# New duration estimates in the clock that writes a trunk kernel's program order

## The chip, the cores and the metric

The kernel runs on one core of a Trainium2 chip. The core's engines run side by side, each through its own instructions in the order in which the program holds them: TensorE (PE) multiplies matrices and writes to PSUM, VectorE (DVE), ScalarE (ACT) and GpSimd (POOL) work on elements, and SyncE (SP) issues DMA transfers. They wait for each other with semaphores. The metric is the device time of one execution in microseconds (us), as the median of several runs. A profiled execution stands beside them: its span runs from the first to the last instruction, and its own time is a little longer than the span.

## The reference

Two layers of an encoder trunk on 512 tokens of 1024 channels, in float32. Each layer is, in short:

```
h = rms_norm(x); proj = h @ w_in          # split into latents, GQA q/k/v, pool channels, 3 gates
o_mla  = latent attention (8 heads, 96-wide q and k, RMS norm per head, rotary part)
o_gqa  = grouped-query attention (8 heads, 2 kv heads, 64 wide, RMS norm per head, rotary)
o_pool = (centred means over 2/4/8/16 tokens - token) @ w_pool * pool_scale
merged = sum over branches of sigmoid(gate_b) * (o_b @ w_branch_b)
x = x + merged @ w_out
u = depthwise_conv3(rms_norm(x) @ w_up) + bias     # 2 * 2816 channels
x = x + (silu(u_gate) * u_val) @ w_down
```

## The kernel before, in words

**Number format.** Every large product is made of three matmuls. Each operand is split into a rounded high part and a low part (ACT makes hi, then DVE or POOL makes lo = x - hi), and high x high, high x low and low x high are added in PSUM. So each weight piece of 128 x 512 costs one DMA share, one ACT copy (wh) and one subtraction (wl). `w_split` (line 302) writes these two, and `wnext` (line 333) keeps them LA = 2 pieces ahead of the matmuls.

**Stages of a layer.** The input projection runs as latents, pool channels, GQA queries, then GQA keys and values. Then comes the GQA attention, with the pool branch's gates and branch products mixed in, as well as the MLA queries and keys; then the MLA attention, mixed with the GQA branch's gates and products and the MLA values; then the MLA branch's gates and products, the output projection, the up-projection with the convolution (`up_evac`, line 1300), and the down-projection.

**The planner's clock.** The program order is not fixed by the loops alone. While the Python code writes the program, `Clock` (line 118) simulates it. Each matmul moves the clock's `now` on by its length. Work behind a matmul is given as a `chain` (line 168): a list of steps, each written into the program when the simulated clock reaches the end of the step before. `took` (line 133) books a cost on an engine: it starts at the later of now (plus a semaphore's delay) and the time at which that engine is free. `Engine` (line 189) wraps the calls to DVE, ACT and POOL and gives each a cost of a fixed part plus so much for each element of a row: `_two` (line 211) is the cost of instructions with two inputs and of reductions, and `tensor_scalar`, `tensor_copy` and `reciprocal` (lines 226 to 234) have their own. `done` and `need` mark results and move the clock to them. None of these costs is an instruction; they only decide what is written when, and so in what order each engine finds its instructions.

Three decisions hang on the clock:

- `pick` (line 317) gives the subtraction of a weight piece (bias W_BIAS = 2.54) or of a probability block (P_BIAS = 1.16) to DVE if DVE is free early enough, otherwise to POOL. `copy` (line 455) chooses between ACT and DVE.
- In `attention` (line 1021) a plan holds, for each head, the positions of its steps: transposes of the query (`t_q`, `t_pair`) and key (`t_k`), the four row-maximum products (`s_max`, line 1098, matmul ps_S, then DVE's reduction nm), the row of maxima (`m_row`), the probabilities (`probs`: matmul ps_ST, exponential pe, its high part ph and low part pl) and the products with the values (`av_hi`, `av_lo`, PSUM bank AV). The position of step p says how many units of filler (gates and branch products, three to six matmuls each) go ahead of it: `fill.upto(target)`.
- Beyond that target, `waiting` (line 1243) asks the clock whether the step's inputs and PSUM bank are ready. As long as they aren't, further units of filler are written first, up to SLACK = 35 units over the target:

```
fill.upto(target)
while fill.done < target + SLACK and waiting(fn, *args) and fill.step():
    pass
fn(*args)
```

PSUM has eight banks: two each for `acc` (projections and filler), `ST` and `AV`, one each for `S` and `mi`.

**Inverse square roots.** `rsqrt_steps` (line 406) makes 1/sqrt on DVE for the norms: one bit operation and three Newton steps of three instructions, ten instructions on rows of 8 or 32 elements, written as one block (`go`). Seven such blocks stand in a layer (two for the token norms, one each for the latents, the GQA queries and keys, the MLA queries and the MLA keys).

## Time and profile before

| | |
|---|---|
| median of 3 runs | 1695.26 us (1694.22 to 1695.61) |
| profiled execution | 1693.48 us, span 1691.7 us |
| mean granted TensorE clock | 0.995 |
| busy: PE, DVE, ACT, POOL | 1649.7, 946.2, 775.4, 962.6 us |
| PE busy, GQA attention of layer 1 (100 to 220 us) | 109.27 of 120.00 us |
| PE busy, MLA attention of layer 1 (242 to 370 us) | 127.88 of 128.00 us |
| PE busy, up-projection of layer 1 (442 to 729 us) | 287.00 of 287.00 us |

A row of the timeline gives start, length, engine, line, operation, tiles (out<-in) and, in brackets, the idle time before it and who ended it. A row of waits gives the total, the number and the longest. A row of stages gives the stretch, its length, then the busy time and the number of instructions of PE, PEld (weight loads), DVE, ACT and POOL, the granted clock as a share of full speed, the DMA share and GB/s. A row of groups gives busy us and the mean ns of one instruction. Most instructions bear the line of the helper that records them: L341 is a matmul, L216 and L220 are two-input instructions, L224 a reduction, L209 an ACT instruction.

### The profile page before, as it was taken

Reading aid. Unit: us, or ns where it says so; the run is one execution under the profiler, and the core shown is the slowest. Engines: PE = TensorE matmul, PEld = TensorE weight load, DVE = VectorE, ACT = ScalarE, POOL = GpSimd, SP = SyncE. Lnnn points to the kernel's source line nnn. Section 1 sums busy time; section 2 is a strip of 40 time slices with the busy share of each in tenths; the row PEclk is TensorE's granted clock in tenths of the full one; section 3 lists DMA queues with packets and bytes.
Section 4 is the critical chain, followed back from the end, with each engine's and each line's share of the span. In section 5 each row is a group of like instructions: output and inputs, shape, how many; then the busy total and the mean of one; then the engine's idle time right before and its main releaser. Section 6 shows DMA issues by size and latency. Waiting matters only on the chain.

```text
span 1691.7 us, 20364 instructions
## 1 busy us (share of the span) xinstructions
PE 1649.7 (98%) x7360; PEld 1336.5 (79%) x7360; DVE 946.2 (56%) x1520; ACT 775.4 (46%) x1361; POOL 962.6 (57%) x759
## 2 busy tenths in 40 slices
PE   8989989999999999999999998999999999999999
PEld 7777667778888888888887786777888888888887
DVE  7776966643357666630157769666433666667100
ACT  5357645653344444432334575456434444444221
POOL 4435645764566656655544466556645665666543
PEclk9999999999999999999999999999999999999999
DMA  4221111113323232333332211111233222222331
GB/s 172 91 72 57 56 48 50 38 63 112 125 88 96 92 100 90 98 109 116 100 106 79 81 44 57 62 38 38 81 115 116 88 100 99 88 97 90 112 119 56
DMA packets 44596, 145.40 MB, mean 86 GB/s; under 512 B 5072, under 2 KB 6352, under 8 KB 44496
## 3 DMA queue, kind: packets, MB, share of 16 engines
q1 hardware_dynamic: 44352, 144.10, 25.7%
q8 instruction: 58, 0.95, 0.2%
q14 instruction: 42, 0.34, 0.1%
q10 hardware_dynamic: 144, 0.01, 0.0%
HBM read 139.90 MB, written 4.19 MB: 85 GB/s over the span
## 4 chain that ended last, share of the span: by engine, by line
PE 89%; DVE 6%; issue 2%; ACT 1%; POOL 1%; DMA 1%; SPq 0%; POOLq 0%; ACTq 0%; DVEq 0%
PE ps_acc L341 40%; PE ps_ST L341 23%; PE ps_AV L341 22%; PE ps_S L341 2%; PE ps_mi L345 1%; PE ps_mi L341 1%; DVE MQ L216 1%; POOL wl L216 1%; DVE yt L220 1%; DVE rp L216 1%; DVE nm L224 1%; DVE osum L236 0%; DVE ssm L224 0%; DVE tabg L216 0%; DMA raw<-w 0%
## 5 line engine op out<-in xcount | busy, mean ns | idle before, releaser
L216 POOL TENSOR_TENSOR wl<-raw,wh 128x512 fp32r<-128x512 f32 (+1 forms) x514 | 680.4, 1333 | 493.5 <-ACT wh L209 437.1
L209 ACT ACTIVATE wh<-raw 128x512 fp32r<-128x512 f32 (+3 forms) x522 | 313.7, 607 | 189.7 <-PE ps_ST L341 87.8
L220 DVE SCALAR_TENSOR_TENSOR a<-u,prm,a 128x512 f32<-128x512 f32 x176 | 242.3, 1377 | 79.8 <-ACT a L209 74.2
L341 PE MATMUL ps_acc<-HH,wh 128*128 128x512 f32 x592 | 236.2, 399 | 5.0 <-DVE XM L220 4.4
L341 PE MATMUL ps_acc<-HH,wl 128*128 128x512 f32 x592 | 234.9, 397 | 0.0
L341 PE MATMUL ps_acc<-HL,wh 128*128 128x512 f32 x592 | 234.9, 397 | 0.0
L216 POOL TENSOR_TENSOR pl<-pe,ph 128x512 fp32r<-128x512 f32 x109 | 143.1, 1313 | 114.2 <-ACT ph L209 77.9
L341 PEld LDWEIGHTS ps_acc<-HH,wh 128*128 128x128 f32 x592 | 112.5, 190 | 33.2 <-ACT wh L209 4.9
L341 PEld LDWEIGHTS ps_acc<-HH,wl 128*128 128x128 f32 x592 | 112.3, 190 | 26.3
L341 PEld LDWEIGHTS ps_acc<-HL,wh 128*128 128x128 f32 x592 | 112.5, 190 | 25.4
L209 ACT ACTIVATE pe<-ps_ST 128x512 f32<-128x512 f32 x128 | 76.1, 594 | 115.9 <-PE ps_ST L341 114.4
L224 DVE TENSOR_REDUCE nm<-ps_S 128x1 fp32r<-128x512 f32 x128 | 87.8, 686 | 55.5 <-PE ps_S L341 55.2
L341 PE MATMUL ps_AV<-HH,wh 128*128 128x512 f32 x288 | 113.8, 395 | 0.0
L341 PE MATMUL ps_AV<-HH,wl 128*128 128x512 f32 x288 | 113.7, 395 | 0.0
L341 PE MATMUL ps_AV<-HL,wh 128*128 128x512 f32 x288 | 113.7, 395 | 0.0
L216 POOL TENSOR_TENSOR al<-a,ah 128x512 fp32r<-128x512 f32 x44 | 58.1, 1321 | 84.8 <-ACT ah L209 58.5
L341 PE MATMUL ps_ST<-HH,wh 128*128 128x512 f32 x240 | 94.9, 395 | 0.0
L341 PE MATMUL ps_ST<-HH,wl 128*128 128x512 f32 x240 | 94.8, 395 | 0.0
L341 PE MATMUL ps_ST<-HL,wh 128*128 128x512 f32 x240 | 94.7, 395 | 0.0
L209 ACT ACTIVATE a<-u,prm 128x512 f32<-128x512 f32 x88 | 71.7, 815 | 27.6 <-DVE u L216 27.3
L209 ACT ACTIVATE ah<-a 128x512 fp32r<-128x512 f32 x44 | 27.8, 631 | 117.5 <-DVE u L240 112.0
L209 ACT ACTIVATE a<-a 128x512 f32<-128x512 f32 x44 | 27.8, 632 | 115.4 <-DVE u L240 115.4
(339 smaller groups left out, 3551.2 us busy)
## 6 DMA issues: line engine op xcount, KB each, us to landing
raw<-w SPq DMA_DIRECT2D x228, 512.0 KB, 3.4
raw<-w SPq DMA_DIRECT2D x13, 384.0 KB, 2.9
XM<-x SPq DMA_DIRECT2D x16, 256.0 KB, 3.8
raw<-w SPq DMA_DIRECT2D x6, 448.0 KB, 3.3
xsp<-XM SPq DMA_DIRECT2D x8, 256.0 KB, 2.0
XM<-xsp SPq DMA_DIRECT2D x8, 256.0 KB, 3.1
out<-XM SPq DMA_DIRECT2D x8, 256.0 KB, 2.4
raw<-w SPq DMA_DIRECT2D x4, 432.0 KB, 3.0
```

The lines of the kernel that those rows point to most:

```text
L209: return self.eng.activation(out, in_, func, **k)
L216: return self.eng.tensor_tensor(out, *a)
L220: return self.eng.scalar_tensor_tensor(out, *a)
L224: return self.eng.tensor_reduce(out, in_, *a, **k)
L341: PE.matmul(o, lhsT=lhsT, rhs=rhs, start=start, stop=stop)
L345: PE.transpose(o, src, ident)
```

## The change

All edits are to the planner's estimates. DVE instructions whose data inputs all lie in SBUF are booked with a wait for POOL: if POOL is booked beyond DVE's start, DVE starts up to 0.62 us later, and POOL's booking moves back by DVE's cost. POOL's two-input instruction gets 0.033 us more, POOL's `tensor_scalar` a cost of its own, the reciprocal less for each element, and each inverse square root 1.2 us more. The constants W_BIAS, P_BIAS, SLACK and the plan's positions stay as they are.

```
-    def took(self, engine, cost):
+    def took(self, engine, cost, port=False):
         start = self.now + (0.0 if self.source is None else 0.13 if self.source == engine else self.SEM)
-        self.free[engine] = max(start, self.free.get(engine, 0.0)) + cost
+        start = max(start, self.free.get(engine, 0.0))
+        if port:
+
+            pool = self.free.get("Pool", 0.0)
+            if pool > start:
+                start += min(0.62, pool - start)
+                self.free["Pool"] = max(pool, start) + cost
+        self.free[engine] = start + cost
...
-    def _count(self, ap, per, fixed):
+    def _count(self, ap, per, fixed, *ins):
...
-        self.ck.took(self.kind, fixed + per * n)
+        port = self.kind == "DVE" and len(ins) > 0 and all(x.space == bass.MemoryType.SB for x in ins)
+        self.ck.took(self.kind, fixed + per * n, port)
...
-    def _two(self, out):
-        self._count(out, *((0.002145, 0.127) if self.kind == "Pool" else (0.00105, 0.07)))
...
+    def _two(self, out, *ins):
+        self._count(out, *((0.002145, 0.16) if self.kind == "Pool" else (0.00105, 0.07)), *ins)
...
-    def tensor_scalar(self, out, *a):
-        self._count(out, 0.00055, 0.07)
...
+    def tensor_scalar(self, out, x, *a):
+        self._count(out, *((0.0043, 0.2) if self.kind == "Pool" else (0.00055, 0.07)), x)
...
     def tensor_copy(self, out, in_, psum=False):
-        self._count(out, 0.00105 if psum else 0.00053, 0.07)
+        self._count(out, 0.00105 if psum else 0.00053, 0.07, in_)
...
     def reciprocal(self, out, in_):
-        self._count(out, 0.0084, 0.07)
+        self._count(out, 0.0066, 0.07)
...
             for to in (y, y, a):
                 newton(to)
+            ck.free["DVE"] += 1.2
+            ck.fin = ck.free["DVE"]
```

`tensor_tensor` and `scalar_tensor_tensor` pass their two data inputs on to `_two`; `tensor_reduce` passes none, so that it never waits for POOL in the clock.

More of the change, by code (lines that the diff above doesn't have):

```diff
@@ L209, in activation, with tensor_tensor, scalar_tensor_tensor @@
         return self.eng.activation(out, in_, func, **k)
-    def _two(self, out):
-        self._count(out, *((0.002145, 0.127) if self.kind == "Pool" else (0.00105, 0.07)))
-    def tensor_tensor(self, out, *a):
-        self._two(out)
-        return self.eng.tensor_tensor(out, *a)
-    def scalar_tensor_tensor(self, out, *a):
-        self._two(out)
-        return self.eng.scalar_tensor_tensor(out, *a)
+    def _two(self, out, *ins):
+        self._count(out, *((0.002145, 0.16) if self.kind == "Pool" else (0.00105, 0.07)), *ins)
+    def tensor_tensor(self, out, x, y, *a):
+        self._two(out, x, y)
+        return self.eng.tensor_tensor(out, x, y, *a)
+    def scalar_tensor_tensor(self, out, x, c, y, *a):
+        self._two(out, x, y)
+        return self.eng.scalar_tensor_tensor(out, x, c, y, *a)
     def tensor_reduce(self, out, in_, *a, **k):
@@ L224, in tensor_reduce @@
         return self.eng.tensor_reduce(out, in_, *a, **k)
-    def tensor_scalar(self, out, *a):
-        self._count(out, 0.00055, 0.07)
-        return self.eng.tensor_scalar(out, *a)
+    def tensor_scalar(self, out, x, *a):
+        self._count(out, *((0.0043, 0.2) if self.kind == "Pool" else (0.00055, 0.07)), x)
+        return self.eng.tensor_scalar(out, x, *a)
     def tensor_copy(self, out, in_, psum=False):
-        self._count(out, 0.00105 if psum else 0.00053, 0.07)
+        self._count(out, 0.00105 if psum else 0.00053, 0.07, in_)
         return self.eng.tensor_copy(out, in_)
     def reciprocal(self, out, in_):
-        self._count(out, 0.0084, 0.07)
+        self._count(out, 0.0066, 0.07)
         return self.eng.reciprocal(out, in_)
```

## The prediction

> **What bounds the kernel now.** I read the page's busy shares first, then PE's waits, then busy time by stage, then the timeline around the longest gaps.

> ```profile
> span 1691.7 us, 20364 instructions
> ...
> PE 1649.7 (98%) x7360; PEld 1336.5 (79%) x7360; DVE 946.2 (56%) x1520; ACT 775.4 (46%) x1361; POOL 962.6 (57%) x759
> ```

> The kernel is a stream of matmuls: PE is busy for all but 1691.7 - 1649.7 = 42.0 us, and no edit touches a matmul. Only two things can move: those 42 us, and the speed at which PE runs after a gap. PE's waits say whom the gaps belong to (total, times, longest):

> ```profile
> PE ps_S L341 <- DVE nm L224: 13.0, 5, 4.2
> PE ps_acc L341 <- ACT wh L209: 4.9, 1, 4.9
> PE ps_acc L341 <- DVE XM L220: 4.4, 3, 2.1
> PE ps_ST L341 <- DVE gqr L216: 4.1, 2, 2.0
> ```

> The largest is the S bank (one PSUM bank for the row maxima), freed by DVE's reduction nm: 13.0 us in five gaps. The 4.9 is the first load and split, which no estimate moves much; the 4.1 lies where PE's order is fixed, behind DVE's four query rotations in a row, and I leave it. By stage (PE, PEld, DVE, ACT, POOL busy, then clock):

> ```profile
> 100.00:220.00 120.00, 109.27 (x488) 85.94 (x487) 91.27 (x155) 73.66 (x134) 65.05 (x51) 0.97 0.17 53
> 242.00:370.00 128.00, 127.88 (x596) 101.77 (x595) 77.43 (x115) 72.04 (x128) 83.88 (x75) 1.00 0.17 53
> 442.00:729.00 287.00, 287.00 (x1241) 232.93 (x1240) 179.81 (x270) 127.74 (x206) 178.68 (x131) 1.00 0.30 95
> 960.00:1075.00 115.00, 108.05 (x475) 84.65 (x474) 88.55 (x140) 74.99 (x133) 68.33 (x54) 0.97 0.15 49
> ```

> In the GQA attention of both layers (100 to 220, 960 to 1075) PE idles 10.7 and 7.0 us; in the MLA attention (242 to 370) and the up-projection (442 to 729) it is full. The change can win or lose in the former, and lose in the latter.

> **The change part by part.** It computes nothing new. The planner's clock decides three things: the order of instructions on each in-order engine, how many filler units go ahead of an attention step (waiting, upto), and which engine takes a split or copy (pick, copy). So each edit is priced by whether the planner now sees a wait that it missed. On the chip no wait is added, and the weight loads on SP's queue keep their order, three slots ahead of the splits. The new cost of tensor_scalar on POOL is nothing here, since no call makes one.

> *The inverse square root (+1.2 us) and the port waits inside it.* This is one such block in front of the longest gap, on DVE, POOL and PE:

> ```profile
> 212.74 0.18 DVE L228 TENSOR_SCALAR y<-ssm 128x32 int32<-128x32 int32 x1
> ...
> 213.18 1.23 DVE L220 SCALAR_TENSOR_TENSOR yt<-yt,y 128x32 f32<-128x32 f32 x1
> ...
> 217.77 0.19 DVE L220 SCALAR_TENSOR_TENSOR ssm<-yt,y 128x32 f32<-128x32 f32 x1
> 217.88 0.68 DVE L224 TENSOR_REDUCE nm<-ps_S 128x1 fp32r<-128x512 f32 x1
> ```
> ```profile
> 213.06 2.73 POOL L216 TENSOR_TENSOR pl<-pe,ph 128x512 fp32r<-128x512 f32 x2 [2.99 <-ACT ph L209]
> ```
> ```profile
> 218.62 0.80 PE L341 MATMUL ps_S<-ka,qa 128*128 128x512 f32 x1 [4.22 <-DVE nm L224]
> ```

> An instruction of 0.19 us takes 1.23 when POOL holds SBUF; the reduction, which reads PSUM, doesn't (0.68). [...]

> The block takes 217.88 - 212.74 = 5.14 us. The old planner reckons 0.088 + 9 x 0.104 = 1.02, so it is 4.1 us short, and the gap is 4.22. The new one reckons 1.02 + 1.2 = 2.22, and up to twice 0.62 more if a POOL instruction is queued: 2.2 to 3.5. That the 1.2 is right where POOL is quiet is seen here (90.63 - 88.50 = 2.13):

> ```profile
> 88.50 0.17 DVE L228 TENSOR_SCALAR y<-ssr 128x32 int32<-128x32 int32 x1
> ...
> 90.63 0.74 DVE L220 SCALAR_TENSOR_TENSOR opl<-ps_AV,prm,oph 128x512 fp32r<-128x512 f32 x1
> ```

> The shortfall drops to 1.7 to 2.9; the planner sees the S bank busy, steps filler in front of s_max, and the 4.2 shrinks by 1.3 to 2.5. I take 1.9. The query block ahead of it:

> ```profile
> 175.24 0.18 DVE L228 TENSOR_SCALAR y<-ssm 128x32 int32<-128x32 int32 x1
> ...
> 179.41 0.68 DVE L224 TENSOR_REDUCE nm<-ps_S 128x1 fp32r<-128x512 f32 x1
> ```
> ```profile
> 180.13 0.50 PE L341 MATMUL ps_S<-ka,qa 128*128 128x512 f32 x1 [1.98 <-DVE nm L224]
> ```

> 4.17 us, 3.15 short, of which the queue hid 1.2. A shortfall of 0.7 to 1.95 leaves 0 to 0.75 of gap: 1.6 saved. Both blocks stand in both layers: 2 x 3.5 = 7.0. The rest of the 13.0 comes from two-input work on MQ, now also reckoned with a wait: 0.4 taken, of 1.0. **Together -7.4** (bounds 0, if no filler is free at that place, and -13.0).

> *The clock behind a gap* (PE busy and clock of 5 us):

> ```profile
> 115.00:120.00 5.00, 4.62 (x18) 4.00 (x17) 1.93 (x3) 3.19 (x6) 0.06 (x1) 0.71 0.33 105
> 215.00:220.00 5.00, 1.38 (x3) 1.16 (x4) 4.83 (x10) 0.00 (x0) 2.01 (x2) 0.69 0.00 0
> 220.00:225.00 5.00, 5.00 (x16) 3.80 (x15) 3.28 (x6) 1.54 (x3) 1.99 (x2) 0.63 0.10 14
> 1020.00:1025.00 5.00, 5.00 (x18) 3.82 (x18) 4.62 (x6) 2.38 (x4) 3.44 (x3) 0.75 0.16 66
> 1055.00:1060.00 5.00, 3.71 (x9) 2.97 (x10) 4.17 (x9) 1.54 (x3) 0.86 (x1) 0.66 0.36 105
> ```

> (1 - clock) x PE busy is 0.4 + 1.9 + 1.3 + 1.3 = 4.9 us behind the S gaps, and 1.3 at 115. If the gaps halve, half of the 4.9 goes: **-2.4** (0 to -4.9). [...]

> *DVE's SBUF costs ahead of the GQA attention.*

> ```profile
> 107.54 0.63 ACT L209 ACTIVATE gt<-gt 128x512 f32<-128x512 f32 x1 [7.68 <-DVE gt L216]
> 108.08 0.92 ACT L209 ACTIVATE wh<-raw 128x384 fp32r<-128x384 f32 x2
> 108.91 2.39 ACT L209 ACTIVATE ka<-ps_mi 64x512 fp32r<-64x512 f32 x4
> ```
> ```profile
> 113.58 0.47 PE L341 MATMUL ps_acc<-HH,wh 128*128 128x512 f32 x1 [2.13 <-DVE XM L220]
> ```

> ACT stood 7.68 us behind a tanh whose input DVE made late, with two weight splits (0.92 us) and the ka copies queued behind it; DVE then waited for ka, and the product that frees PE's bank stood behind that. With DVE's lateness known, the tanh is written later and the two splits ahead of it: about 0.9 of 2.1 us a layer, 1.8, and a little clock. **-2.0** (+3 if the order falls out worse, -6 if gap and clock loss go).

> *Costs of POOL and the reciprocal.* POOL's instruction goes from 0.127 + 512 x 0.002145 = 1.225 to 1.258 and is pushed back by each overlapping DVE instruction; the reciprocal drops from 1.145 to 0.915; DVE's two-input instruction stays 0.608, plus up to 0.62:

> ```profile
> L220 DVE SCALAR_TENSOR_TENSOR a<-u,prm,a 128x512 f32<-128x512 f32 x176 | 242.3, 1377 | 79.8 <-ACT a L209 74.2 <-POOL wl L216 1.3 <-POOL al L216 1.0
> ...
> L236 DVE RECIPROCAL osum<-osum 128x128 f32<-128x128 f32 x64 | 58.1, 931 | 6.1 <-ACT osum L209 5.9
> ```

> 1.23 and 0.915 are near the traced 1.377 and 0.931. In the up-projection this may send a few weight splits to DVE: DVE has 287 - 180 = 107 us free there and PE's order is fixed, so **nothing**; without that cover each would cost at most its own 1.3 us.

> *Everything shifts.* The new clock reorders all stages that pick or fill. Each reordered stage can get gaps of its own; I add **+3.0** for them, an estimate between 0 (the MLA attention, 242 to 370, has next to none) and +11 (what the GQA attention of layer 1 idles now), nearer to the former since the old, less exact clock also left most stages full.

> Sum: -7.4 - 2.4 - 2.0 + 3.0 = -8.8 against the profiled execution's 1693.48 (span 1691.7 and 1.8 around it): 1684.7. The median of the runs lies 1.8 above the profiled one, so **1686.5**.

> **The rivals.**
> *Filler runs dry (slower).* Filler stepped early is missing later. At position 28, where the last head's probabilities begin, (32.0 - 28)/(32.0 + 1.9) of some 92 units, about 11, are left.

> ```profile
> L209 ACT ACTIVATE pe<-ps_ST 128x512 f32<-128x512 f32 x128 | 76.1, 594 | 115.9 <-PE ps_ST L341 114.4
> ```

> If overruns eat more than 11 units, the exponential, its copy (as long again) and the split (0.6 + 0.6 us, and 2.73/2 by the POOL row above) of the last head lie bare: some 3 us with the matmuls around them, and 2 of clock as above. In all four attentions that is +20, on top of -8.8: 1706; in three, 1701. For: SLACK allows 35 units. Against: the two blocks' foreseen waits, 2.5 to 5 us, are 4 to 8 units of 0.64 us (three matmuls at 127.88/596).
> *The wait only moves (no change).* DVE is near full at the gaps (4.83 of 5.00 us above): PE's S step, put later, meets the next late reduction. Then gains and new gaps about cancel: 1692 to 1698.
> *Full cover.* All S gaps, the XM gaps and 6.2 us of clock go: -13.0 - 4.4 - 6.2 = -23.6: 1671.7. Against: the 0.62 cap.
> *Not doing what it says.* The blocks' steps are seen but s_max keeps its place, since SLACK or the target forbids filler: as "no change".

> **How the numbers follow.** Forecast (-4 to -16) 0.50, full cover 0.06, no change of either kind 0.15, filler dry 0.29. Within 0.2% (3.4 us, about what a measurement can tell from no change) is 0.15; faster 0.56; slower 0.29. The range leaves out half of full cover and the worse part of the dry case: 1674 to 1703; the forecast's own is 1679 to 1691.

> **What would show it.** Right: PE's wait for nm falls from 13.0 to about 5.6 with none over 3 us; more filler (ps_acc<-HH, oph) ahead of the S matmuls at 175 and 212; clock above 0.97 in the GQA stage; up-projection unchanged with PE full. Wrong: gaps at the ends of attentions, PE waiting for pl or ph, or DVE over 80% there through splits moved to it.

## The result and the profile after

The median of the kernel after is 1697.34 us (1695.82 to 1703.18) against 1694.30 (1691.49 to 1695.75) for the kernel before, run beside it: a ratio of 1.0026, interval 1.0018 to 1.0035. It is a little slower, where the prediction had 1686.5 and faster. The profiled execution took 1696.52 us, 3.0 more than that of before. Its page begins:

```profile
span 1694.7 us, 20363 instructions
...
PE 1650.7 (97%) x7360; PEld 1334.8 (79%) x7360; DVE 944.0 (56%) x1516; ACT 784.3 (46%) x1372; POOL 974.2 (57%) x752
```

PE idles 1694.7 - 1650.7 = 44.0 us, where it idled 42.0. The total hardly moved, but its make-up did. PE's waits after (total, number, longest; the change shifts the lines, so that a matmul now bears L349, two-input instructions L224 and L228, a reduction L232 and an ACT instruction L217):

```profile
PE ps_acc L349 <- ACT wh L217: 6.3, 3, 5.0
PE ps_acc L349 <- DVE XM L228: 5.7, 4, 3.5
PE ps_S L349 <- DVE nm L232: 5.7, 5, 1.8
PE ps_ST L349 <- DVE gqr L224: 5.5, 2, 2.7
PE ps_AV L349 <- POOL pl L224: 2.4, 4, 0.6
...
PE ps_AV L349 <- DVE ph L240: 1.6, 2, 1.0
PE ps_AV L349 <- ACT ph L217: 1.6, 3, 0.7
```

The S bank's row (nm) fell from 13.0 to 5.7, with nothing over 1.8 us: the gain that was forecast is there. All else that PE waits for rose from 42.0 - 13.0 = 29.0 to 44.0 - 5.7 = 38.3 us. New are pl and ph (5.6 together); XM (the gated products) and gqr (the rotated GQA queries) grew by 1.3 and 1.4. By stage (length, busy time of PE, PEld, DVE, ACT and POOL, clock, DMA share, GB/s):

```profile
100.00:220.00 120.00, 112.57 (x508) 89.24 (x507) 90.01 (x151) 78.99 (x143) 67.45 (x52) 0.99 0.17 53
242.00:370.00 128.00, 126.54 (x586) 100.10 (x585) 77.39 (x111) 73.19 (x129) 82.16 (x72) 1.00 0.16 48
442.00:729.00 287.00, 287.00 (x1241) 232.63 (x1240) 173.06 (x271) 127.82 (x206) 185.76 (x130) 1.00 0.31 95
960.00:1075.00 115.00, 104.82 (x461) 80.32 (x460) 92.92 (x136) 73.53 (x130) 65.30 (x52) 0.99 0.17 51
...
209.03:212.44 3.41, 3.41 (x10) 2.33 (x10) 2.97 (x10) 1.93 (x4) 1.30 (x1) 0.50 0.00 0
922.42:925.83 3.41, 2.89 (x10) 2.60 (x10) 3.10 (x13) 1.02 (x2) 0.10 (x1) 0.50 0.00 0
1041.89:1045.30 3.41, 3.41 (x13) 2.92 (x12) 3.41 (x6) 1.23 (x2) 0.37 (x1) 0.50 0.18 73
```

Layer 1's GQA attention gained 3.3 us of PE time (109.27 to 112.57) and its clock rose from 0.97 to 0.99. The MLA attention lost 1.3 us, layer 2's GQA attention 3.2. The up-projection is full, as before. The last three rows are the stretches in which the clock was halved.

**Where the gain went.** Three places show it. The longest new gap is at 1041 us in layer 2; PE and DVE around it:

```profile
1037.71 0.28 PE L349 MATMUL ps_acc<-wh,ctl 128*128 128x256 f32 x1
1041.45 0.47 PE L349 MATMUL ps_acc<-HH,wh 128*128 128x512 f32 x1 [3.46 <-DVE XM L228]
```
```profile
1037.91 0.69 DVE L232 TENSOR_REDUCE nm<-ps_S 128x1 fp32r<-128x512 f32 x1
1038.62 1.28 DVE L224 TENSOR_TENSOR rp<-MQ,tabm 128x256 f32<-128x256 f32 x1
1039.82 0.94 DVE L244 RECIPROCAL osum<-osum 128x128 f32<-128x128 f32 x1
1040.69 0.62 DVE L228 SCALAR_TENSOR_TENSOR XM<-gt,ps_acc 128x512 f32<-128x512 f32 x1
```

The waiting matmul is filler. XM is the gated product that reads a finished filler piece out of its acc bank, and DVE, without a pause before it, comes to it last. The reduction nm (1037.91) isn't what PE lacks any more; a later result of the same full DVE is. That the S product was put later and the filler in its place met DVE's queue is how theory 2 below would have it; it was not followed step by step.

Of the two S gaps of 1.8 us that are left, the one at 1018.95 us still stands behind an inverse square root, whose block takes 6.5 us there. The other (PE, last fence) stands behind the rotation of a key (DVE, then POOL):

```profile
206.04 1.36 DVE L224 TENSOR_TENSOR krr<-krt,tabm 128x128 f32<-128x128 f32 x1
207.33 0.68 DVE L232 TENSOR_REDUCE nm<-ps_S 128x1 fp32r<-128x512 f32 x1
...
208.52 0.28 DVE L224 TENSOR_TENSOR krr<-krr,rp 128x128 f32<-128x128 f32 x1
```
```profile
206.00 1.26 POOL L224 TENSOR_TENSOR wl<-raw,wh 128x512 fp32r<-128x512 f32 x1
```
```profile
208.06 0.50 PE L349 MATMUL ps_S<-ka,qa 128*128 128x512 f32 x1 [1.80 <-DVE nm L232]
```

A krr instruction (128 rows of 128 elements) takes 1.36 us beside POOL's and 0.28 when POOL is idle again. The difference, 1.08, is more than the 0.62 that the planner may book, so the planner reckons it at least 0.46 too short.

The third place is the end of each attention. This is the last head's work in layer 1's GQA attention:

```profile
231.46 0.73 PE L349 MATMUL ps_AV<-ph,vg 128*128 128x512 f32 x2 [0.67 <-DVE ph L240]
...
233.21 0.50 PE L349 MATMUL ps_AV<-pl,vg 128*128 128x512 f32 x1 [0.54 <-POOL pl L224]
```

No ps_acc matmul stands between the value products there: the filler is spent. In the program order of PE, the units' matmuls left there when the last head's four probability steps begin are 12, 12, 12, 9 in the kernel before, and none in the kernel after.

### The profile page after: what moved, and what is told of

It is laid out like the page before. It is cut to its first block, busy times and chain, and to the rows that moved or that the text cites. A ratio compares the mean times of both kernels' runs of the same rounds, so it can differ in the third digit from the quotient of the medians.

```text
span 1694.7 us, 20363 instructions
## 1 busy us (share of the span) xinstructions
PE 1650.7 (97%) x7360; PEld 1334.8 (79%) x7360; DVE 944.0 (56%) x1516; ACT 784.3 (46%) x1372; POOL 974.2 (57%) x752
## 3 DMA queue, kind: packets, MB, share of 16 engines
q1 hardware_dynamic: 44352, 144.10, 26.9%
## 4 chain that ended last, share of the span: by engine, by line
PE 89%; DVE 6%; ACT 2%; issue 1%; POOL 1%; DMA 1%; SPq 0%; POOLq 0%; DVEq 0%; ACTq 0%
PE ps_acc L349 39%; PE ps_ST L349 23%; PE ps_AV L349 22%; PE ps_S L349 3%; PE ps_mi L349 2%; PE ps_mi L353 1%; POOL pl L224 1%; DVE rp L224 1%; DVE MQ L224 1%; DVE nm L232 1%; ACT pe L217 0%; ACT ph L217 0%; DVE tabg L224 0%; DMA raw<-w 0%; DVE wl L224 0%
## 5 line engine op out<-in xcount | busy, mean ns | idle before, releaser
L224 POOL TENSOR_TENSOR wl<-raw,wh 128x512 fp32r<-128x512 f32 (+3 forms) x512 | 682.8, 1340 | 576.5 <-ACT wh L217 512.6
L217 ACT ACTIVATE wh<-raw 128x512 fp32r<-128x512 f32 (+3 forms) x522 | 315.6, 609 | 207.6 <-PE ps_ST L349 88.6
L228 DVE SCALAR_TENSOR_TENSOR a<-u,prm,a 128x512 f32<-128x512 f32 x176 | 218.3, 1244 | 74.5 <-ACT a L217 71.6
L349 PE MATMUL ps_acc<-HH,wh 128*128 128x512 f32 x592 | 235.2, 397 | 8.3 <-DVE XM L228 5.7
L349 PE MATMUL ps_acc<-HH,wl 128*128 128x512 f32 x592 | 234.4, 396 | 1.7 <-POOL wl L224 1.7
L349 PE MATMUL ps_acc<-HL,wh 128*128 128x512 f32 x592 | 234.0, 395 | 0.0
L224 POOL TENSOR_TENSOR pl<-pe,ph 128x512 fp32r<-128x512 f32 x104 | 139.7, 1345 | 102.0 <-ACT ph L217 68.9
L349 PEld LDWEIGHTS ps_acc<-HH,wh 128*128 128x128 f32 x592 | 111.8, 189 | 35.3 <-issue 3.6
L349 PEld LDWEIGHTS ps_acc<-HH,wl 128*128 128x128 f32 x592 | 111.7, 189 | 29.2 <-POOL wl L224 3.0
L349 PEld LDWEIGHTS ps_acc<-HL,wh 128*128 128x128 f32 x592 | 111.8, 189 | 25.3
L217 ACT ACTIVATE pe<-ps_ST 128x512 f32<-128x512 f32 x128 | 76.1, 595 | 113.2 <-PE ps_ST L349 110.8
L232 DVE TENSOR_REDUCE nm<-ps_S 128x1 fp32r<-128x512 f32 x128 | 87.5, 683 | 54.6 <-PE ps_S L349 54.0
L349 PE MATMUL ps_AV<-HH,wh 128*128 128x512 f32 x288 | 113.8, 395 | 0.0
L349 PE MATMUL ps_AV<-HH,wl 128*128 128x512 f32 x288 | 113.6, 395 | 0.0
L349 PE MATMUL ps_AV<-HL,wh 128*128 128x512 f32 x288 | 113.6, 395 | 0.0
L217 ACT ACTIVATE a<-u,prm 128x512 f32<-128x512 f32 x88 | 71.8, 816 | 55.7 <-DVE u L224 55.7
L349 PE MATMUL ps_ST<-HH,wh 128*128 128x512 f32 x240 | 94.9, 395 | 0.0
L349 PE MATMUL ps_ST<-HH,wl 128*128 128x512 f32 x240 | 94.7, 395 | 0.0
L349 PE MATMUL ps_ST<-HL,wh 128*128 128x512 f32 x240 | 94.7, 395 | 0.0
L217 ACT ACTIVATE ah<-a 128x512 fp32r<-128x512 f32 x44 | 27.8, 631 | 105.5 <-DVE u L248 100.0
L224 POOL TENSOR_TENSOR al<-a,ah 128x512 fp32r<-128x512 f32 x44 | 72.3, 1644 | 5.2 <-ACT ah L217 5.2
L217 ACT ACTIVATE a<-a 128x512 f32<-128x512 f32 x44 | 27.9, 634 | 93.3 <-DVE u L248 87.7
```

What stands on the lines that cost most here:

```text
L217: return self.eng.activation(out, in_, func, **k)
L224: return self.eng.tensor_tensor(out, x, y, *a)
L228: return self.eng.scalar_tensor_tensor(out, x, c, y, *a)
L232: return self.eng.tensor_reduce(out, in_, *a, **k)
L349: PE.matmul(o, lhsT=lhsT, rhs=rhs, start=start, stop=stop)
```

## The experiments

Four theories were stated. **1:** filler runs dry at the ends of attentions. **2:** the wait only moves, since DVE is full at that place. **3:** the loss lies where PE's order is fixed (gqr, the identity matrix idr that DVE rounds at the start, the first splits). **4:** every new order has gaps of its own, whatever the planner knows. "Elsewhere" below is PE's idle time (span less PE busy) without the wait ps_S <- nm. The waits and the clock of a kernel come from its one profiled execution, and a ratio is to the kernel before on the same chip.

### The three parts, alone and in all combinations

The parts are R (the 1.2 us of an inverse square root), P (the booking of DVE's waits for POOL, `port` in the code) and C (the costs of POOL and of the reciprocal). R alone on the kernel before, and C alone on it:

```
             for to in (y, y, a):
                 newton(to)
+            ck.free["DVE"] += 1.2
+            ck.fin = ck.free["DVE"]
```
```
-        self._count(out, *((0.002145, 0.127) if self.kind == "Pool" else (0.00105, 0.07)))
+        self._count(out, *((0.002145, 0.16) if self.kind == "Pool" else (0.00105, 0.07)))
...
-        self._count(out, 0.0084, 0.07)
+        self._count(out, 0.0066, 0.07)
```

R alone:

> The kernel before with the 1.2 us of each inverse square root alone; no waits for POOL are booked. Theory 1 (filler runs dry: the booked waits for POOL make the planner spend the filler early, and the last heads lie bare): here little filler is spent early (6 filler matmuls stand behind the last head's probabilities in the GQA attention, 12 before, 0 after), so PE's waits for nm shrink by 3 to 6 us of 13.0 and no waits for ph or pl come: 2 to 5 us faster than before, 1689 to 1692. Theory 2 (the wait only moves, because DVE is full there and the filler itself waits for DVE's product): PE's wait for XM grows by as much as that for nm shrinks: within 2 us of before.

C alone:

> The kernel before with the new costs of POOL and of the reciprocal alone. If the edits' effects add (the costs made the kernel with the 1.2 us alone 2.3 us longer), 1696.5 +- 1. If each order has gaps of its own (theory 4), anything from 1692 to 1702, with PE's wait for nm still at 12 to 15 us, since nothing tells the planner of the slow inverse square roots, and no waits for ph or pl. The prediction's term for these costs, nothing, would be 1693.5 to 1695.5.

P alone (the kernel after without the two lines of R and with the old costs):

> The changed kernel without the 1.2 us and with the old costs of POOL and the reciprocal: the booked waits for POOL alone. Theory 1: the filler is spent as early or earlier (0 filler matmuls behind the last head's probabilities in all four attentions), so PE waits for ph and pl at least 5 us in all, and the time is 3 to 10 us above before: 1697 to 1704. Theory 2: as the changed kernel or better, within 3 us of before, with the loss in XM.

R and C:

> The kernel before with the 1.2 us and the new costs of POOL and the reciprocal, no waits for POOL booked: the whole change but for the one edit that theory 1 blames. Theory 1: filler is left everywhere (6 matmuls behind the last GQA probabilities, 15 to 27 in MLA), 2 to 5 us faster than before, as with the 1.2 us alone: 1689 to 1692. Rival: all reorderings cost some 3 us, whichever edit makes them: 1694 to 1697.

R and P:

> The 1.2 us and the port waits, with the old costs. It completes the eight combinations of the three parts. If effects add, 1692.0 + 17.3 = 1709, like the port waits alone less 2.5. If the loss of the port waits comes from filler spent early (theory 1), this kernel books the most waits of all on POOL and must show waits for ph and pl of 5 us or more, and lie above 1700. If each order has gaps of its own (theory 4), the 17.3 isn't a property of the port waits, and it may as well lie at 1695 to 1700, with waits in places that none of the others shows.

P and C (the kernel after without the two lines of R):

> The changed kernel without the 1.2 us, new costs of POOL and the reciprocal kept. Theory 1: with the waits for POOL booked the last heads lie bare with or without the 1.2 us, but the waits for nm grow back by 3 to 6 us: 1700 to 1704. The rival, that the 1.2 us only helps where the rest is as before, has it within 2 us of the changed kernel.

| kernel | median us | ratio to before, interval | nm | elsewhere | clock |
|---|---|---|---|---|---|
| before | 1694.30 | | 13.0 | 29.0 | 0.995 |
| R | 1691.98 | 0.9989 (0.9980 to 0.9998) | 4.6 | 34.4 | 0.996 |
| C | 1700.07 | 1.0036 (1.0023 to 1.0049) | 19.3 | 25.2 | 0.989 |
| P | 1711.77 | 1.0102 (1.0085 to 1.0118) | 10.0 | 41.6 | 0.993 |
| R, C | 1694.29 | 1.0001 (0.9992 to 1.0009) | 14.2 | 26.9 | 0.993 |
| R, P | 1704.08 | 1.0058 (1.0046 to 1.0070) | 4.4 | 42.8 | 0.998 |
| P, C | 1696.22 | 1.0008 (0.9999 to 1.0016) | 8.9 | 33.6 | 0.996 |
| R, P, C (after) | 1697.34 | 1.0026 (1.0018 to 1.0035) | 5.7 | 38.3 | 0.997 |

Against the expectations: R has the time of theory 1 (1689 to 1692), and its wait for XM didn't grow as theory 2 had it (3.4). C has a time that theory 4 allows, with more of nm than expected. P lies 8 us above the range of theory 1. R and C, and P and C, lie where the rivals of theory 1 had them. R and P fits theory 1: above 1700, with 7.5 us of pl and ph.

The times don't add: C costs 5.8 us on the kernel before and wins 15.6 on P. Nor does R always win: on P and C it costs 1.1. The waits are steadier, though they leave out PE's busy time, which moves as well, in good part with the clock (1649.7 before, 1657.8 with P, 1658.1 with C). R takes 3.2 to 8.4 us off nm in each of its four pairs. **The port booking adds 8.4 to 12.6 us of waiting elsewhere in each of its four pairs** (41.6 - 29.0, 42.8 - 34.4, 33.6 - 25.2, 38.3 - 26.9), and takes 0.2 to 10.4 off nm. On top of R and C, as in the change, it wins 8.5 and loses 11.4. P alone shows where:

```profile
PE ps_S L349 <- DVE nm L232: 10.0, 7, 2.4
PE ps_ST L349 <- DVE gqr L224: 5.5, 2, 2.7
...
PE ps_AV L349 <- POOL pl L224: 4.0, 8, 0.6
...
PE ps_AV L349 <- ACT ph L217: 3.3, 4, 1.3
```

and R alone has neither pl nor ph, and gqr as before, while qb (the row of maxima, written beside a query's low part) took up some of what nm left, 1.1 before and 4.4 now:

```profile
PE ps_S L341 <- DVE nm L224: 4.6, 4, 1.7
PE ps_ST L341 <- DVE qb L216: 4.4, 4, 2.0
PE ps_ST L341 <- DVE gqr L216: 4.1, 2, 2.0
```

So on the kernel before, the whole forecast gain in nm comes with R alone, without the port booking's price, though 5.4 us of it come back elsewhere. Beside C it doesn't: R and C has 14.2, and in the change it is the port booking that takes nm from there to 5.7.

### Does the filler that runs dry cost the time?

SLACK at 6 in place of 35, in the kernel after and in the kernel before, and six units that steps beyond the target may not touch:

```
-    SLACK = 35
+    SLACK = 6
```
```
-                while fill.done < target + SLACK and waiting(fn, *args) and fill.step():
+                while fill.done < min(target + SLACK, fill.total - 6) and waiting(fn, *args) and fill.step():
```

After, SLACK 6:

> The changed kernel with SLACK 6 in place of 35, so that filler can be written at most 6 units ahead of its target; behind the last head's probabilities 9 to 15 (GQA) and 9 to 21 (MLA) filler matmuls are left. Theory 1: PE's 5.6 us of waits for ph and pl vanish, a part of the waits for nm comes back (5.7 to perhaps 8 us): 3 to 8 us faster than the changed kernel, 1689 to 1694. Theory 2: DVE is as full as ever, the loss goes back from XM to nm: within 2 us of the changed kernel, about 1697.

Before, SLACK 6:

> The kernel before with SLACK 6, as the control. Theory 1: before isn't dry, so the limit only takes cover away from waits that the old clock foresees: 0 to 4 us slower than before. Theory 2: the same.

After, six units kept:

> The changed kernel, in which the step that writes filler beyond its target leaves the last 6 units alone; up to the last head of each attention the order of PE is the changed kernel's, but for 2 units. Behind the last head's probabilities 9 to 18 (GQA) and 12 (MLA) filler matmuls are left, against 0 and 0 to 12. Theory 1 (the last heads lie bare): PE's 5.6 us of waits for ph and pl go, and little else moves: 3 to 7 us faster than the changed kernel, 1690 to 1694. Theory 4 (every new order has gaps of its own, whatever makes it): the ph and pl waits go, but others come; 1694 to 1700.

Measured: 1695.55 (ratio 1.0006, 0.9997 to 1.0014), 1707.01 (1.0083, 1.0069 to 1.0097) and 1697.09 (1.0016, 1.0007 to 1.0025). The kernel after gains 1.8 and 0.3 us, where theory 1 had 3 to 8 and 3 to 7. With SLACK 6 its waits for pl and ph, 5.6 us, are gone altogether, and yet PE idles 43.5 us against 44.0, since other waits came in their place. With six units kept:

```profile
PE ps_mi L349 <- DVE nm L232: 3.2, 3, 2.0
PE ps_AV L349 <- POOL pl L224: 2.5, 4, 0.7
```

The 3.2 us of ph are gone, but PE's wait for the row of maxima (ps_mi <- nm) rose from 1.0 to 3.2. The bare ends exist, and covering half of them moves the wait to an earlier head (the longest, 2.0 us, lies at 1055.6 us, 20 us ahead of the end). Theory 1 has the mechanism right and not the price: it isn't the net cause. In the kernel before, the small SLACK costs 12.7 us, where both theories had 0 to 4, so long steps past the target are worth much there.

### Where the port booking hurts, and which half of it

`took` books port waits only while `ck.port_on` is set; it is set outside the attentions only, or inside only:

```
-        if port:
+        if port and self.port_on:
```

Outside only:

> The changed kernel, with the waits for POOL booked everywhere but in the two attentions of each layer. Theory 1 (filler runs dry in the attentions): filler is left behind the last head's probabilities (3 matmuls in GQA, 15 to 27 in MLA, against 0 and 0 to 12), so no waits for ph or pl: 4 to 8 us faster than the changed kernel, 1689 to 1693. Theory 3 (the loss lies in the stages with a fixed PE order, where the waits for gqr, idr and the splits behind 100 us grew by some 4 us in all): these waits stay as in the changed kernel, and it is at least as slow as before: 1694 to 1698.

Inside only:

> The changed kernel, with the waits for POOL booked in the attentions alone. Theory 1: the filler is spent as early as in the changed kernel, PE waits for ph and pl some 5 us, and the time is that of the changed kernel or worse: 1696 to 1702. Theory 3: the waits for gqr and idr go back to before, the time falls by about 4 us: 1692 to 1694.

Then each half of the booking alone, first without POOL's pushed-back booking, then without DVE's later start:

```
                 start += min(0.62, pool - start)
-                self.free["Pool"] = max(pool, start) + cost
```
```
-                start += min(0.62, pool - start)
                 self.free["Pool"] = max(pool, start) + cost
```

DVE's later start only:

> The kernel after, but a booked port wait no longer moves POOL's booking back; DVE's start is still late by up to 0.62 us. Theory 1 (filler stepped early for work booked late on POOL): pl is booked earlier, fewer units go early, waits for ph and pl fall from 5.6 to below 3 us, 1693 to 1695. Theory 2 (DVE full, the wait only moves): the same DVE bookings, so the gaps for XM (5.7) and gqr (5.5) stay, and the time with them, 1696 to 1698. Theory 4: 1692 to 1705 with a new list of waits.

POOL's pushed-back booking only:

> The kernel after, but a booked port wait only moves POOL's booking back; DVE starts as early as in the planner before. Theory 1: POOL is still booked late, waits for ph and pl of 5 us or more stay, 1696 to 1699. Theory 2: DVE's lateness is no longer seen, so its waits come back, nm 8 us or more as without the 1.2 us, XM and gqr as before (4.4, 4.1), 1695 to 1697. Theory 4: 1692 to 1705 with a new list of waits.

Measured: outside only 1708.65 (1.0087, 1.0074 to 1.0100), inside only 1700.57 (1.0036, 1.0023 to 1.0049). Both are worse than the whole, so neither place alone holds the loss. Outside only lies above what every theory had; inside only has 6.1 us of pl and ph and lies in the range of theory 1. In the attentions the booking both takes nm down and adds the most elsewhere: nm and elsewhere are 6.8 and 40.7 inside only, 15.3 and 33.9 outside only, 14.2 and 26.9 without it (R, C). gqr is 5.5 with the booking outside and 4.1 without: its 1.4 us are theory 3's, shown, and small. The halves give 1694.40 (1.0001, 0.9993 to 1.0010) and 1693.23 (0.9993, 0.9984 to 1.0001). DVE's later start alone:

```profile
PE ps_acc L348 <- DVE XM L227: 4.5, 5, 0.9
...
PE ps_AV L348 <- POOL pl L223: 2.4, 4, 0.6
PE ps_AV L348 <- DVE ph L239: 1.9, 2, 1.0
PE ps_AV L348 <- ACT ph L216: 1.8, 4, 0.7
```

It has as much of pl and ph (6.1) as the kernel after and runs 2.9 us faster, which again clears theory 1. It lacks the long XM gap (none over 0.9), but PE idles no less, 44.8 us against 44.0. What it gains is PE's busy time, 1647.7 against 1650.7, as much as its clock explains, 0.999 against 0.997: some 1.7 us of 1692.5 are lost by it, what one halved stretch costs, where the kernel after has three. POOL's half alone, with R and C, has 7.3 of nm and 30.8 elsewhere, where DVE's later start has 7.9 and 36.9. So either half does most of the work on nm, and DVE's later start alone adds 10.0 us elsewhere to the 26.9 of R and C, POOL's half 3.9, both together 11.4. In time the whole booking loses 3 to 4 us against either half. That DVE's later start and POOL's later booking feed each other, so that the planner counts one wait twice, would fit; this is argued, not shown.

### The same clock in another order

A semaphore's delay in the planner, 0.15 us, set to 0.16 or 0.14. It says nothing new about the chip, and it writes another order.

```
-    SEM = 0.15
+    SEM = 0.16
```

Before, 0.16:

> A control: the kernel before, with the planner's semaphore delay at 0.16 us in place of 0.15, a change that means nothing on the chip and only shifts the written order a little; the filler left at each head is the same as in before. Theory 4 (every new order costs, since the plan's positions and biases fit the old one): 2 to 10 us slower than before, 1696 to 1704. Theory 1: within 2 us of before.

R alone, 0.16:

> The same shift of 0.01 us on the kernel before with the 1.2 us alone. If the gain of the 1.2 us is the foreseen wait for nm and not one lucky order, it is 1 to 4 us faster than the kernel before with the same shift. Theory 4: no such difference, either sign up to 5 us.

R alone, 0.14:

> The kernel before with the 1.2 us alone and the planner's semaphore delay at 0.14 in place of 0.15, which means the same and writes another order. If the gain of the 1.2 us alone (2.5 us) belongs to the 1.2 us, 1690.5 to 1693; if it belonged to that one order (theory 4; at 0.16 it was gone), 1693.5 to 1697. In both, PE's wait for nm stays near 5 us.

After, 0.16:

> The same shift of 0.01 us on the changed kernel; the filler is spent as early as there (15 and 6 matmuls at the last head's first row maximum, 0 behind its probabilities). Theory 1: within 2 us of the changed kernel, 1695 to 1699. Theory 4: it can go 5 us either way.

After, 0.14:

> The kernel after with the same shift of the planner's semaphore delay, 0.14. If its loss belongs to the new clock as a whole, it lies at 1697 to 1700 like its two sisters; if to the one order (theory 4), it may as well lie below 1694.5. PE's wait for nm near 6 us, waits for ph and pl near 5.6 in both.

| planner | 0.14 | 0.15 | 0.16 |
|---|---|---|---|
| before | not run | 1694.30 | 1693.86, 0.9994 (0.9985 to 1.0003) |
| R alone | 1686.83, 0.9951 (0.9939 to 0.9964) | 1691.98 | 1694.49, 0.9999 (0.9991 to 1.0008) |
| after | 1694.68, 1.0004 (0.9995 to 1.0013) | 1697.34 | 1699.60, 1.0030 (1.0019 to 1.0042) |

The same planner spreads over 7.7 us (R) and 4.9 us (after), though only 0.4 us over the two orders of before, where theory 4 had 2 to 10. So the 3.0 us between before and after are less than what a meaningless shift does to two of the three planners, and theory 4 holds as to size. Nor does R gain in every order: at 0.16 it is no faster than before. But at each of the three delays, the full change lies 5.1 to 7.9 us above R alone. R at 0.14 beats both kernels, at about the time that had been forecast for the change; that it does so in this order and not in its neighbours is luck. Its page and waits:

```profile
span 1684.1 us, 20357 instructions
...
PE 1648.0 (98%) x7360; PEld 1330.8 (79%) x7360; DVE 947.9 (56%) x1526; ACT 775.0 (46%) x1359; POOL 962.0 (57%) x755
```
```profile
PE ps_S L341 <- DVE nm L224: 4.4, 7, 1.3
...
PE ps_acc L341 <- DVE XM L220: 2.2, 4, 0.9
```

It idles 36.1 us, and its clock is 0.999. It looks as the forecast described: nm near 5 us, no long gap in the attentions, one halved stretch of the clock (0.66 from 90 to 95 us), and nothing given back at their ends but 1.1 us for pl.

## Why the prediction was wrong, by its own steps

*The inverse square root and the port waits, -7.4.* Right in size for nm: 13.0 to 5.7, so -7.3. The mechanism, filler written ahead of a row maximum that is seen to be late, is shown for R alone, and for the change only in layer 2. With R alone the two blocks of layer 1 take 4.3 and 4.2 us (4.2 and 5.2 before), 9 and 6 filler matmuls (ps_acc) start during them in place of 3 and 3, and the gaps behind them fall from 1.98 and 4.22 us to

```profile
180.13 0.50 PE L341 MATMUL ps_S<-ka,qa 128*128 128x512 f32 x1 [0.58 <-DVE nm L224]
...
218.90 0.50 PE L341 MATMUL ps_S<-ka,qa 128*128 128x512 f32 x1 [1.71 <-DVE nm L224]
```

In the kernel after, 12 and 15 start during the blocks of layer 2. In layer 1 there are 3 and 3 as before, so more filler isn't what closed the gaps there. The blocks themselves are shorter, 2.2 and 2.8 us, and POOL is busy for 0.00 and 0.70 us during them, where it was for 2.50 and 3.86 before:

```profile
172.67 0.18 DVE L236 TENSOR_SCALAR y<-ssm 128x32 int32<-128x32 int32 x1
...
174.69 0.19 DVE L228 SCALAR_TENSOR_TENSOR ssm<-yt,y 128x32 f32<-128x32 f32 x1
...
211.06 0.74 DVE L236 TENSOR_SCALAR y<-ssm 128x32 int32<-128x32 int32 x1
...
213.64 0.19 DVE L228 SCALAR_TENSOR_TENSOR ssm<-yt,y 128x32 f32<-128x32 f32 x1
```

For the forecast that is luck: it had the blocks as long as before. Whether the port booking or chance moved POOL's splits away is not shown. One row of the prediction is read wrongly: the reduction at 217.88 us runs when POOL is done (at 217.01), so its 0.68 us show nothing of a reduction beside POOL; the one at 181.21 us, with POOL's instruction from 181.36 beside it, took 0.68 us too. That POOL "holds SBUF" is the prediction's reading: the rows show 1.23 us for a DVE instruction at 213.18 with POOL's from 213.06 beside it, and 0.19 us for those from 217.09 on, when POOL is idle, and not by what means. The prediction also didn't ask what the port booking would do everywhere else.

*The clock behind a gap, -2.4.* Nearly right in sum. The clock was at 0.50 in four stretches before, from 115, 217, 1019 and 1057 us, and in three after. PE is busy for 15.35 and 9.71 us in them, of which half is lost: 7.7 and 4.9 us, so -2.8. Behind S gaps the loss fell from 6.0 (4.9 by the prediction's rows of 5 us) to 1.7, more than forecast, but 1.4 came new behind gqr in layer 2 and 1.7 behind the new XM gap.

*DVE's SBUF costs ahead of the GQA attention, -2.0.* The place answered by about as much, in another order. ACT's idle time before the tanh fell from 7.68 to 2.87 us, but the two splits now stand behind the ka copies, not ahead of them:

```profile
107.09 0.63 ACT L217 ACTIVATE gt<-gt 128x512 f32<-128x512 f32 x1 [2.87 <-DVE gt L224]
107.98 2.41 ACT L217 ACTIVATE ka<-ps_mi 64x512 fp32r<-64x512 f32 x4 [0.26 <-PE ps_mi L353]
110.41 1.15 ACT L217 ACTIVATE wh<-raw 128x512 fp32r<-128x512 f32 x2
```
```profile
111.09 0.50 PE L349 MATMUL ps_acc<-HH,wh 128*128 128x512 f32 x1 [0.69 <-ACT wh L217]
112.46 0.50 PE L349 MATMUL ps_acc<-HH,wl 128*128 128x512 f32 x1 [0.63 <-POOL wl L224]
```

The 2.13 us gap became 0.69 + 0.63, and that of layer 2 went from 2.15 to 0.67 + 0.63: 1.7 us saved, and the halved stretch at 115 us is gone too (it is counted under the clock). The total for XM hides this, since 5.7 us came new at other places, 3.46 of them at 1041 us.

*Costs of POOL and the reciprocal, nothing.* Wrong as a separate edit, and by a way not thought of. The up-projection stayed full as argued, but C alone made the kernel 5.8 us slower. In its profiled execution nm rose to 19.3, yet PE's idle time as a whole only from 42.0 to 44.5; the clock, 0.989 against 0.995, is the larger part. That the nearer cost took away an error which had made up for another one is only argued.

*Everything shifts, +3.0.* **This is the step that failed:** the price of the new order was put at 3.0 us and measured 14.8, above its upper bound of 11. Waits other than nm rose by 9.3 us although 1.7 were saved ahead of the attention, so new gaps cost 11.0. And PE's busy time rose by 1.0 although the clock gave 2.8 back, so PE was 3.8 us slower in other ways. The sum in its new form is -7.3 - 2.8 - 1.7 + 11.0 + 3.8 = +3.0, what the two spans differ by.

The 3.8 belong to the gaps as well, for the most part. There are ten more gaps over 0.15 us (37 against 27), and the first 128x512 matmul behind one takes 0.47 or 0.50 us in the rows above, against 0.39 in an unbroken run (as at 1035.04 us in the kernel after; the means on its page for ps_acc are 0.395 to 0.397). An estimate from the starts of all matmuls in the two traces, each against the usual distance for its shape, puts some 2.3 us at the gaps, beyond their idle time, and in the two matmuls behind each, and 1.1 in further pauses too short for the list of waits. The rest stays open.

The term was put near the low end of 0 to +11 on the ground that the old clock left most stages full. That says how good the one old order is, and not how good a new one will be. The table of the eight combinations shows what was to be asked: the port booking makes PE wait 8.4 to 12.6 us more elsewhere whatever it is combined with.

*The rivals.* "The wait only moves" was given 1692 to 1698 and, with its sister without any change, a share of 0.15; the time lies there, and at 1041 us PE is seen to wait for the next result of a full DVE. "Filler runs dry" reckoned with 11 units left for the last head, where the kernel before has 12 matmuls, four units of three. It was seen as well, in all four attentions, but at 5.6 us in all and not 20: the gaps are 0.2 to 1.0 us each, and the three halved stretches all lie elsewhere. "Full cover" was far off, as the prediction's own word against it, the 0.62 cap, already said.

What stays open is why one order has the 3.46 us gap in layer 2 and its neighbour not (after, 0.14: XM 2.1 us in all, longest 1.3), and so why the planner's new order has the gaps that it has. The planner's steps were not followed that far.

## What to carry to other kernels

In a kernel whose order is written by a simulated clock, a truer cost is not by itself a gain: try it alone and in several orders of equal meaning before it is believed, since here such orders differ by up to 7.7 us and the whole change by 3. Price a new order by what else waits, above all for the engine that was found full: R alone took 8.4 us of waits for nm away and gave 5.4 back elsewhere, most of it in waits for other results of DVE. Correct the one cost that the longest gap names first (here the inverse square root, which put the time at 1686.8, 1692.0 and 1694.5 us in three orders, against 1693.9 and 1694.3 without it), and add general corrections one by one, with a look at the total idle time of PE each time.

## What the runs showed of the hardware

*In the kernel after, the clock fell behind a gap of 1.80 us, and not behind one of 2.74.* The 1.80 us gap that ends at 208.06 us is followed by 3.41 us at a clock of 0.50, from 209.03 us: 1.7 us lost. The 2.74 us gap behind gqr in layer 1 is followed by no drop:

```profile
87.57 0.50 PE L349 MATMUL ps_ST<-mxh,wh 128*128 128x512 f32 x1 [2.74 <-DVE gqr L224]
```
```profile
87.00:92.00 5.00, 4.43 (x31) 4.30 (x32) 4.69 (x15) 1.84 (x4) 1.87 (x2) 1.00 0.33 107
```

Whether it is also where a gap falls on the raster that makes the runs of one kernel differ is not shown. Of the 18 runs of the kernel after, seven took 1700.4 to 1703.2 us at a mean clock of 0.993 to 0.995, and the others 1695.8 to 1698.7 at 0.995 to 0.998.
